# Sums of raw weights, attention's causal mask and half the rotations move from VectorE to GpSimd; inner operands are prepared in two pairs

## The chip, the cores and the metric

The kernel runs on one core of one Trainium2 chip. The metric is the device time of one execution in microseconds (us), the median of several. The engines are called as in the profile: PE (TensorE's matmuls) and PEld (its weight loads), DVE (VectorE), ACT (ScalarE), POOL (GpSimd), SP (SyncE, which issues the DMAs).

## What is computed

Two layers over 1024 tokens of width 1024 in float32. The first layer mixes by sliding-window attention with sinks, the second by a gated recurrence (HGRN2); each is followed by an MLP with a squared ReLU of inner width 4096. Cut to what matters here:

```python
# attention: blocks of 128 queries see their own block (causal) and the block before
q, k = apply_partial_rotary(q, cos, sin), apply_partial_rotary(k, cos, sin)   # 16 of 64 columns of a head
mask = (delta >= 0) & (delta < WINDOW) & (key_pos >= 0)
probs = softmax_with_sink(where(mask, q @ k.T * HEAD_DIM ** -0.5, NEG_INF), sink)
x = x + (probs @ v) @ w_o
...
# recurrence: q, f, i, g = split(h @ w_in, 4); chunks of 64 tokens with a carried state
...
# both layers
h = rmsnorm(x, mlp_norm[layer])
x = x + square(relu(h @ w_up[layer])) @ w_down[layer]
```

## The kernel before

Float32 accuracy is reached by three fast products: each operand is split into a high part (`wh` for weights, made by a cast on ACT or DVE) and a low part (`wl`, a subtraction on DVE), and `mm3` adds high x high, high x low and low x high. On top of that the large products are done by Strassen's scheme in Winograd's form: a 2 x 2 block product takes seven products instead of eight, and needs sums of blocks of the weights (s1 to s4) and of the activations.

`strassen_weights` loads four raw weight tiles of 128 x 512 (`wr`, by DMA), makes s1 = a10 + a11, s2 = s1 - a00, s3 = a00 - a10, s4 = a01 - s2 in tiles called `m`, and splits all of them into `wh` and `wl`. `pair` uses it for one pair of the up product's output tiles, 16 pairs in each layer; `two` uses it for the recurrence's projections, 12 times. From the fifth pair on, products 2 and 4 of a pair are not done directly: `inner` does them for two pairs at a time, ahead of use, by a second Strassen level on halves of 256 columns, with its own four half-width sums in each of 6 calls for each of the two products and each layer. `prepare` makes the activation sums that `inner` needs: it reads four kept tiles back by DMA, subtracts halves, splits three of the results and writes all of them to DRAM by DMA. `put_in` puts one more into place in pair 3 (pairs are counted from 0).

In attention, `attend_block` computes 4 heads x 128 queries x 256 keys, transposes the probabilities on PE, copies them to SBUF with ACT (`y`) and multiplies a copy by a 0/1 triangle `own_t` to keep keys up to the query (`own`); both feed the value products on PE. `rope` rotates a block's queries or keys by two products with the tables and a difference and a sum.

The order on each engine is not the written one. Every operation is recorded with the engines that may do it and a planned cost (`Schedule.add`); due times are worked back from PE's order, and a list scheduler (`Schedule.order`) then fills the engines by rank, with weight work given a lead. Where two engines may do an operation (casts to `wh`: ACT or DVE) it takes the one that looks better by the planned loads. Buffers come from small pools (`BUFS`): 6 `wr`, 5 `wh`, 5 `wl`, 7 `m`. On the chip each engine then runs its list in order. All instructions carry the line of the one call that issues them (L374), so they are told apart by tile names. PSUM banks are `p` and `q`, activation tiles `a` and `t`, DRAM tiles `d`, constants `c`.

Of the kernel before, what the change touches and what calls it, by code (L numbers as in the profile page):

```python
# [15 lines left out]
ALU = mybir.AluOpType  # L16
AX = mybir.AxisListType

P = 128
# [12 lines left out]
NG = 4  # L32
HD = 64
ROT = 16
# [9 lines left out]
LEVELS = 6  # L44
WARM = 10
INNER = (2, 4)
AT = 2
K_SPANS = ((-1, 3), (2, 6), (5, 8))

# [271 lines left out]
class Net:  # L321
# [88 lines left out]
        self.s.add({e: ways[e] for e in engines}, [out], [in_])  # L410

    def tt(self, e, out, x, y, alu, n=TH):
        cost = {"DVE": 70 + n * 1.04, "Pool": 147 + n * 2.105}
        engines = ("DVE",) if e == "any" else (e,)
        ways = {e: self.call(self.engine(e).tensor_tensor, out, x, y, alu) + (cost[e],) for e in engines}
        self.s.add(ways, [out], [x, y])
# [217 lines left out]
    def strassen_weights(self, first, second, done=()):  # L634

        self.s.lead = LEAD
        a = {(i, k): self.raw(src[:, k * TH : k * TH + TH]) for i, src in enumerate((first, second)) for k in range(2)}
        s1, s2, s3, s4 = (self.t(tag="m") for _ in range(4))
        self.tt("any", s1, a[1, 0], a[1, 1], ALU.add)
        self.tt("any", s2, s1, a[0, 0], ALU.subtract)  # L640
        self.tt("any", s3, a[0, 0], a[1, 0], ALU.subtract)
        self.tt("any", s4, a[0, 1], s2, ALU.subtract)
        order = ((1, a[0, 0]), (5, s1), (2, a[0, 1]), (6, s2), (3, s4), (7, s3), (4, a[1, 1]))
        w = {name: self.weight_split(z) for name, z in order if name not in done}
        self.s.lead = 0
        return w

    def prepare(self, name):

        near, far = slice(0, TH // 2), slice(TH // 2, TH)  # L650
        u = [self.t() for _ in range(HK)]
        for z, kept in zip(u, self.quarters[name]):
            self.dma(z, kept, 4 * P * TH)
        yield
        made = self.quarters[name] = {}

        def difference(out, x, y):
            for i in range(2):
                self.tt("any", out[:, i].only(i), x(i), y(i), ALU.subtract, TH // 2)

        def stored(k, t):
            made[k] = [self.keep(z.bitcast(F32)) for z in self.split(t.rearrange("p i c -> p (i c)"), self.t)]

        low, high = (lambda c: lambda i: u[i][:, c]), (lambda c: lambda i: u[2 + i][:, c])
        new = lambda: self.t(F32, (P, 2, TH // 2))
        part = lambda t: lambda i: t[:, i].only(i)
        t1 = new()
        difference(t1, low(far), low(near))
        made[5] = self.keep(t1.rearrange("p i c -> p (i c)"))
        yield  # L670
        t2 = new()
        difference(t2, high(far), part(t1))
        stored(6, t2)
        yield
        t3 = new()
        difference(t3, high(far), low(far))
        stored(7, t3)
        yield
        t4 = new()
        difference(t4, high(near), part(t2))  # L680
        stored(4, t4)
        yield
# [13 lines left out]
    def inner(self, name, m, x, y):  # L696
# [4 lines left out]
        a0, a1 = (self.raw(self.io["up"][self.layer, i + row * (MT // 2)][:, TH:]) for i in (m, m + 1))  # L701
        sa, sb = self.t(tag="m"), self.t(tag="m")
        s1, s2, s3, s4 = sa[:, near].only(0), sa[:, far].only(1), sb[:, near].only(0), sb[:, far].only(1)
        self.tt("any", s1, a1[:, near], a1[:, far], ALU.add, half)
        self.tt("any", s2, s1, a0[:, near], ALU.subtract, half)
        self.tt("any", s3, a0[:, near], a1[:, near], ALU.subtract, half)
        self.tt("any", s4, a0[:, far], s2, ALU.subtract, half)
        wide = []
        w = {1: (0, near), 2: (0, far), 5: (1, near), 6: (1, far), 7: (2, near), 3: (2, far), 4: (3, far)}
        self.s.lead = 0  # L710
        banks = [self.psum(), self.psum()]
        main, side, own = banks[0][:, near].only(0), banks[1][:, near].only(0), banks[1][:, far].only(1)

        def product(k, ps, start):
            more = {} if start else {"skip_group_check": True}
# [110 lines left out]
    def mlp(self, cut):  # L826

        x = self.mlp_second()
        made, n = {}, MT // 2
        for m in range(n):  # L830
            between, first = [], m - m % 2
            if m == AT:
                between += [self.prepare(name) for name in INNER]
            if m == AT + 1:
                between += [self.put_in(name, x[name]) for name in INNER]
            for name in INNER:
                c = first if name == 4 else first + 2
                if AT < c < n and m % 2 == (name == 2):
                    made[name, c] = []
                    between.append(self.inner(name, c, x, made[name, c]))  # L840
            done = {name: made[name, first][m % 2] if name == 2 else lambda: made[4, first][m % 2] for name in INNER if (name, first) in made}
            if m == n - 2:
                self.r = [self.a() for _ in range(NH)]
                for hf in range(NH):
                    self.copy(self.r[hf], self.spread(self.square[hf]))
            if m == 1 and self.layer == 0:
                self.hgrn_constants()
            self.pair(m, x, done, between)
        yield from self.down(cut)
# [175 lines left out]
        self.neg = self.const((P, 1))  # L1025
        self.memset(self.neg, NEG)

    def rope(self, x, heads, n):
        half = ROT // 2
        v = x.rearrange("p (h d) -> p h d", d=HD)[:, :, :ROT].rearrange("p h (a r) -> p h a r", a=2)  # L1030
        prod = []
        for tab in self.trig:
            y = self.t(F32, (P, 8, 2, half))[:, :heads]
            tb = tab[:, n].unsqueeze(1).unsqueeze(1).to_broadcast([P, heads, 2, half])
            self.tt("any", y, v, tb, ALU.mult, heads * ROT)
            prod.append(y)
        yc, ys = prod
        self.tt("any", v[:, :, 0], yc[:, :, 0], ys[:, :, 1], ALU.subtract, heads * half)
        self.tt("any", v[:, :, 1], yc[:, :, 1], ys[:, :, 0], ALU.add, heads * half)

    def k_tiles(self, i):
        if self.ks[i] is None:
# [34 lines left out]
    def projected(self, cg, n, ps, r):  # L1077
        if cg == 0:
            self.keys_values(n, ps, r)
        else:  # L1080
            q = self.a()
            self.stt(halves(q), straight(ps), r, halves(self.bias[cg]), ALU.mult, ALU.add)
            self.rope(q, 8, n)
            self.q[n][cg - 1] = q

    def keys_values(self, n, ps, r):
# [9 lines left out]
        if n:  # L1096
            before = self.v[(n - 1) // 2][:, (n - 1) % 2].only(n - 1)
            self.tt("any", self.dv[n // 2][:, n % 2].only(n), v, before, ALU.subtract, W)
        self.rope(k, NG, n)
        pk = self.psum("q")[:, : 2 * P].rearrange("p (g s) -> p g s", g=2)  # L1100
        for gp in range(2):
            self.transpose(pk[:, gp], k[:, gp * P : gp * P + P])
# [52 lines left out]
    def attend_block(self, g, n, stacks):  # L1155
# [30 lines left out]
        if n:  # L1186
            y = self.t(F32, (P, 4, P))
            self.copy(y, pt)
            self.tt("any", own, y, mask, ALU.mult)
            parts = [(y, self.v[(n - 1) // 2].only(n - 1)[:, (n - 1) % 2, g * HD : g * HD + HD]),  # L1190
                     (own, self.dv[n // 2].only(n)[:, n % 2, g * HD : g * HD + HD])]
        else:
            self.tt("DVE", own, pt, mask, ALU.mult)
            parts = [(own, v)]
# [536 lines left out]
```

## Time and profile before

| | |
|---|---|
| Time, median of 3 runs (lowest to highest) | 1993.26 us (1992.43 to 1994.49) |
| Profiled execution: time, span | 1992.46 us, 1990.6 us |
| Granted PE clock | 0.998 |
| DVE, ACT, POOL busy | 1763.1, 1108.4, 61.9 us |
| HBM traffic | 205 GB/s over the span |

An engine's busy time is set against the span. The profile has no stage names; by the tiles that are worked on, attention runs to about 330 us, the first up product to about 600, the first down product to about 1000, the recurrence to about 1350, with its output product and the second MLP behind it.

### The profile page before, as it was taken

To read this page: it belongs to the slowest core of one execution; us is meant where nothing else is said; L and a number is where in the kernel's file an instruction comes from. 1 tells how busy PE (TensorE), PEld (TensorE's weight loads), DVE (VectorE), ACT (ScalarE), POOL (GpSimd) and SP (SyncE) were. 2 spreads that over 40 slices of the span, in tenths; PEclk is the share of its full clock that TensorE was granted. 3 is DMA by queue.
4 is the path that set the end of the run, shared out by engine and by line. 5 is a ranking of instruction groups with operands and counts; after the bars stand their busy time and mean duration, and the time that the engine had idled before them with its cause. 6 is when DMAs were issued, how large, how long until landed. Compare 5 with 4: busy or idle time off the path is not lost.

```text
span 1990.6 us, 34667 instructions
## 1 busy us (share of the span) xinstructions
PE 1968.2 (99%) x11836; PEld 1723.3 (87%) x11836; DVE 1763.1 (89%) x3557; ACT 1108.4 (56%) x2280; POOL 61.9 (3%) x124
## 2 busy tenths in 40 slices
PE   9999999999999999999999999999999999999998
PEld 8877788899998888888888888888889998888887
DVE  8999899898889878899899999989989888987787
ACT  6567797666664423355455555554766666343352
POOL 4030000000000000000000000000000000000001
PEclk9999999999999999999999999999999999999999
DMA  6211464998889977755412212667599888986752
GB/s 224 90 54 59 127 217 162 308 304 290 285 264 319 330 244 244 242 167 179 140 59 81 75 60 86 206 203 253 185 313 305 285 278 280 317 315 211 239 173 85
DMA packets 232401, 411.04 MB, mean 206 GB/s; under 512 B 25504, under 2 KB 35744, under 8 KB 232224
## 3 DMA queue, kind: packets, MB, share of 16 engines
q1 hardware_dynamic: 231648, 408.30, 62.0%
q8 instruction: 93, 1.52, 0.3%
q14 instruction: 84, 0.69, 0.1%
q10 hardware_dynamic: 576, 0.52, 0.1%
HBM read 305.97 MB, written 102.76 MB: 205 GB/s over the span
## 4 chain that ended last, share of the span: by engine, by line
PE 89%; DVE 6%; issue 2%; ACT 2%; DMA 1%; POOL 0%; POOLq 0%; SPq 0%; DVEq 0%; ACTq 0%
PE q L374 51%; PE p L374 39%; DVE t L374 2%; DVE a L374 1%; DVE wl L374 1%; DVE m L374 1%; ACT t L374 1%; ACT a L374 1%; ACT wh L374 0%; ACT m L374 0%; DMA wr<-in_wo 0%; POOL a L374 0%; DMA wr<-in_up 0%; DMA a<-in_x 0%; DMA d<-t 0%
## 5 line engine op out<-in xcount | busy, mean ns | idle before, releaser
L374 PE MATMUL q<-a,wh 128*128 128x512 f32 x2368 | 708.4, 379 | 1.9 <-ACT t L374 1.6
L374 PE MATMUL p<-a,wh 128*128 128x512 f32 (+1 forms) x2304 | 657.7, 365 | 0.9 <-DVE wh L374 0.8
L374 PEld LDWEIGHTS q<-a,wh 128*128 128x128 f32 x2368 | 438.8, 189 | 59.2 <-ACT t L374 2.4
L374 PEld LDWEIGHTS p<-a,wh 128*128 128x128 f32 x2304 | 421.1, 189 | 55.4 <-issue 1.2
L374 PE MATMUL q<-a,wl 128*128 128x512 f32 x1184 | 448.1, 379 | 0.0
L374 PE MATMUL p<-a,wl 128*128 128x512 f32 (+1 forms) x1152 | 418.4, 364 | 0.0
L374 ACT CAST a<-t 128x512 fp32r<-128x512 f32 (+1 forms) x299 | 178.8, 613 | 216.8 <-PE q L374 126.6
L374 DVE TENSOR_TENSOR t<-t,t 128x512 f32<-128x512 f32 (+3 forms) x424 | 256.0, 628 | 11.6 <-ACT t L374 10.3
L374 PEld LDWEIGHTS q<-a,wl 128*128 128x128 f32 x1184 | 223.9, 189 | 30.3
L374 DVE TENSOR_TENSOR wl<-wr,wh 128x512 fp32r<-128x512 f32 (+1 forms) x352 | 233.8, 667 | 12.2 <-ACT wh L374 4.7
L374 PEld LDWEIGHTS p<-a,wl 128*128 128x128 f32 x1152 | 218.2, 190 | 25.1 <-issue 0.4
L374 DVE TENSOR_TENSOR a<-t,a 128x512 fp32r<-128x512 f32 (+2 forms) x334 | 218.4, 677 | 0.5 <-ACT a L374 0.2
L374 DVE TENSOR_TENSOR wl<-m,wh 128x512 fp32r<-128x512 f32 x296 | 201.6, 684 | 7.6 <-ACT wh L374 4.0
L374 ACT CAST wh<-wr 128x512 fp32r<-128x512 f32 x221 | 131.7, 598 | 136.1 <-PE p L374 46.2
L374 ACT ACTIVATE t<-t 128x512 f32<-128x512 f32 x296 | 183.7, 630 | 35.7 <-DVE t L374 23.5
L374 ACT CAST wh<-m 128x512 fp32r<-128x512 f32 x239 | 147.0, 618 | 89.5 <-PE p L374 38.8
L374 ACT COPY t<-q 128x512 f32<-128x512 f32 (+3 forms) x190 | 105.2, 557 | 63.8 <-PE q L374 59.3
L374 DVE CAST wh<-wr 128x512 fp32r<-128x512 f32 (+1 forms) x131 | 55.0, 419 | 89.2 <-PE q L374 67.2
L374 ACT COPY t<-p 128x256 f32<-128x256 f32 (+1 forms) x157 | 70.5, 452 | 95.4 <-PE p L374 78.0
L374 DVE TENSOR_TENSOR m<-wr,wr 128x512 f32<-128x512 f32 x184 | 118.8, 649 | 3.8 <-DMA wr<-in_down 3.5
L374 PE MATMUL p<-wh,a 128*128 128x512 f32 x352 | 110.9, 385 | 0.0
L374 PEld LDWEIGHTS q<-t,t 128*64 128x64 f32 (+1 forms) x2160 | 95.5, 144 | 14.0 <-issue 6.3
(138 smaller groups left out, 2330.4 us busy)
## 6 DMA issues: line engine op xcount, KB each, us to landing
t<-d SPq DMA_DIRECT2D x428, 256.0 KB, 4.4
d<-t SPq DMA_DIRECT2D x312, 256.0 KB, 4.1
wr<-in_down SPq DMA_DIRECT2D x256, 256.0 KB, 4.2
wr<-in_up SPq DMA_DIRECT2D x176, 256.0 KB, 4.4
a<-d SPq DMA_DIRECT2D x60, 256.0 KB, 4.9
wr<-in_wqkv SPq DMA_DIRECT2D x48, 256.0 KB, 2.9
d<-a SPq DMA_DIRECT2D x48, 256.0 KB, 3.3
wr<-in_win SPq DMA_DIRECT2D x48, 256.0 KB, 2.9
```

The source lines that it names most:

```text
L374: fn(*[place(a) for a in args], **{k: place(v) for k, v in kw.items()})
```

## The change

Five edits. The four sums of `strassen_weights` and of `inner` are given to POOL instead of DVE. POOL's planned cost of such an operation goes from 147 + 2.105 n to 212 + 3.0 n ns for n columns. `prepare` runs in pair 1 for product 2 and in pair 2 for product 4, where both ran in pair 2 (with it, the record of what was made is set up before the first step). The rotation of the queries of the second half's blocks goes to POOL; keys and the first half stay on DVE. The own-block mask becomes an index selection on POOL (keep where query index minus key index is not negative) in every block but the first. The banks of `inner` are tracked whole instead of by halves.

```diff
 INNER = (2, 4)
+PREPARED = {2: 1, 4: 2}
...
     def tt(self, e, out, x, y, alu, n=TH):
-        cost = {"DVE": 70 + n * 1.04, "Pool": 147 + n * 2.105}
+        cost = {"DVE": 70 + n * 1.04, "Pool": 212 + n * 3.0}
...
     def strassen_weights(self, first, second, done=()):
-        self.tt("any", s1, a[1, 0], a[1, 1], ALU.add)
-        self.tt("any", s2, s1, a[0, 0], ALU.subtract)
-        self.tt("any", s3, a[0, 0], a[1, 0], ALU.subtract)
-        self.tt("any", s4, a[0, 1], s2, ALU.subtract)
+        self.tt("Pool", s1, a[1, 0], a[1, 1], ALU.add)
+        self.tt("Pool", s2, s1, a[0, 0], ALU.subtract)
+        self.tt("Pool", s3, a[0, 0], a[1, 0], ALU.subtract)
+        self.tt("Pool", s4, a[0, 1], s2, ALU.subtract)
...
     def inner(self, name, m, x, y):
-        self.tt("any", s1, a1[:, near], a1[:, far], ALU.add, half)
+        self.tt("Pool", s1, a1[:, near], a1[:, far], ALU.add, half)
...
-        main, side, own = banks[0][:, near].only(0), banks[1][:, near].only(0), banks[1][:, far].only(1)
+        main, side, own = banks[0][:, near], banks[1][:, near], banks[1][:, far]
...
-            if m == AT:
-                between += [self.prepare(name) for name in INNER]
+            between += [self.prepare(name) for name, at in PREPARED.items() if m == at]
...
     def projected(self, cg, n, ps, r):
-            self.rope(q, 8, n)
+            self.rope(q, 8, n, "DVE" if n < BPH else "Pool")
...
     def attend_block(self, g, n, stacks):
-            self.tt("any", own, y, mask, ALU.mult)
+            self.op("Pool", self.nc.gpsimd.affine_select, [own], [y], 750, own, y, [[0, 4], [1, P]], ALU.is_ge, 0.0,
+                    base=0, channel_multiplier=-1)
```

Three places in the built order. First, DVE before at the start of the first up product; the weight sums (`m`) stand between the splits (`wl`) and the activations' sums (`t`).

```order
L374 TENSOR_TENSOR wl_3909<-wr_3772,wh_3896 128x512
L374 TENSOR_TENSOR m_3916<-wr_3824,wr_3855 128x512
L374 TENSOR_TENSOR t_3763<-t_3763,t_3699 128x512
L374 TENSOR_TENSOR a_3931<-p_3862,t_3663 128x512
L374 TENSOR_TENSOR wl_3936<-wr_3795,wh_3922 128x512
L374 TENSOR_TENSOR m_3945<-m_3916,wr_3795 128x512
L374 TENSOR_TENSOR t_3708<-t_3941,t_3708 128x512
L374 TENSOR_TENSOR t_3884<-t_3884,t_3948 128x512
L374 TENSOR_TENSOR m_3969<-wr_3806,m_3945 128x512
L374 TENSOR_TENSOR wl_3976<-m_3916,wh_3961 128x512
```

The same pair's place on DVE now, where a cast to `wh` stands that ACT did before:

```order
L375 TENSOR_TENSOR wl_3955<-wr_3789,wh_3941 128x512
L375 TENSOR_TENSOR t_3889<-t_3889,t_3947 128x512
L375 CAST wh_3972<-m_3907 128x512
L375 TENSOR_TENSOR t_3889<-t_3889,t_3953 128x512
L375 TENSOR_TENSOR wl_3983<-m_3907,wh_3972 128x512
L375 TENSOR_TENSOR t_3889<-t_3889,t_3961 128x512
```

And on POOL now, two pairs' sums in one row, s3, s1, s2, s4 of each:

```order
L375 TENSOR_TENSOR m_3877<-wr_3789,wr_3839 128x512
L375 TENSOR_TENSOR m_3907<-wr_3839,wr_3863 128x512
L375 TENSOR_TENSOR m_3930<-m_3907,wr_3789 128x512
L375 TENSOR_TENSOR m_3958<-wr_3813,m_3930 128x512
L375 TENSOR_TENSOR m_3980<-wr_3893,wr_3924 128x512
L375 TENSOR_TENSOR m_4009<-wr_3924,wr_3966 128x512
```

The sums have left DVE's row; over the whole program 181 casts (156 of 512 columns, 25 of 256) have come to it from ACT.

Second, DVE before in the pair where both preparations ran: the halves' differences (128x256) of both products, mixed with weight sums and splits.

```order
L374 TENSOR_TENSOR m_4599<-wr_4520,wr_4531 128x512
L374 TENSOR_TENSOR t_4536<-t_4492 128x256
L374 TENSOR_TENSOR t_4612<-t_4484 128x256
L374 TENSOR_TENSOR wl_4618<-wr_4307,wh_4602 128x512
L374 TENSOR_TENSOR t_4612<-t_4504 128x256
L374 TENSOR_TENSOR t_4627<-t_4468,t_4536 128x256
L374 TENSOR_TENSOR t_4627<-t_4543,t_4536 128x256
L374 TENSOR_TENSOR m_4635<-m_4599,wr_4307 128x512
L374 TENSOR_TENSOR m_4644<-wr_4307,wr_4520 128x512
```

DVE now, in the pair before that one, with the differences of one product alone:

```order
L375 TENSOR_TENSOR t_4447<-t_4322 128x256
L375 TENSOR_TENSOR t_4447<-t_4302 128x256
L375 CAST wh_4461<-m_4237 128x512
L375 TENSOR_TENSOR wl_4468<-m_4237,wh_4461 128x512
L375 TENSOR_TENSOR t_4474<-t_4408,t_4447 128x256
L375 TENSOR_TENSOR t_4478<-t_4408,t_4322 128x256
L375 TENSOR_TENSOR t_4474<-t_4424,t_4447 128x256
```

The eight differences of one product have moved a pair ahead; those of the other follow 20 rows later on the same engine.

Third, attention, while the second half's queries are projected. DVE before: rotations (products with the tables `c_430` and `c_453`) and the mask (product with `c_103`) among the softmax's steps.

```order
L374 TENSOR_TENSOR t_1982<-a_1869,c_430 128x128
L374 TENSOR_TENSOR t_1985<-t_1971,c_103 128x512
L374 COPY_PREDICATED m_1422<-c_98,q_1966 128x2x128
L374 TENSOR_TENSOR t_1999<-a_1869,c_453 128x128
L374 TENSOR_TENSOR t_2003<-a_1891,c_430 128x128
L374 TENSOR_TENSOR a_1869<-t_1982,t_1999 128x8x8
```

POOL now, at the same place:

```order
L375 TENSOR_TENSOR t_1949<-a_1926,c_430 128x128
L375 TENSOR_TENSOR t_1961<-a_1926,c_453 128x128
L375 TENSOR_TENSOR a_1912<-t_1929,t_1936 128x8x8
L375 AFFINE_SELECT t_1975<-t_1958 128x512
L375 TENSOR_TENSOR a_1912<-t_1929,t_1936 128x8x8
L375 TENSOR_TENSOR t_1997<-a_1956,c_430 128x128
```

The selection of one block stands between the steps of a rotation in POOL's row, so it starts only when those ahead of it have run.

More of the change, by code (lines that the diff above doesn't have):

```diff
@@ L653, in prepare @@
             self.dma(z, kept, 4 * P * TH)
+        made = self.quarters[name] = {}
         yield
-        made = self.quarters[name] = {}
         def difference(out, x, y):
@@ L703, in inner @@
         s1, s2, s3, s4 = sa[:, near].only(0), sa[:, far].only(1), sb[:, near].only(0), sb[:, far].only(1)
-        self.tt("any", s1, a1[:, near], a1[:, far], ALU.add, half)
-        self.tt("any", s2, s1, a0[:, near], ALU.subtract, half)
-        self.tt("any", s3, a0[:, near], a1[:, near], ALU.subtract, half)
-        self.tt("any", s4, a0[:, far], s2, ALU.subtract, half)
+        self.tt("Pool", s1, a1[:, near], a1[:, far], ALU.add, half)
+        self.tt("Pool", s2, s1, a0[:, near], ALU.subtract, half)
+        self.tt("Pool", s3, a0[:, near], a1[:, near], ALU.subtract, half)
+        self.tt("Pool", s4, a0[:, far], s2, ALU.subtract, half)
         wide = []
@@ L1026, in attention_constants, with rope @@
         self.memset(self.neg, NEG)
-    def rope(self, x, heads, n):
+    def rope(self, x, heads, n, e):
         half = ROT // 2
@@ L1034, in rope @@
             tb = tab[:, n].unsqueeze(1).unsqueeze(1).to_broadcast([P, heads, 2, half])
-            self.tt("any", y, v, tb, ALU.mult, heads * ROT)
+            self.tt(e, y, v, tb, ALU.mult, heads * ROT)
             prod.append(y)
         yc, ys = prod
-        self.tt("any", v[:, :, 0], yc[:, :, 0], ys[:, :, 1], ALU.subtract, heads * half)
-        self.tt("any", v[:, :, 1], yc[:, :, 1], ys[:, :, 0], ALU.add, heads * half)
+        self.tt(e, v[:, :, 0], yc[:, :, 0], ys[:, :, 1], ALU.subtract, heads * half)
+        self.tt(e, v[:, :, 1], yc[:, :, 1], ys[:, :, 0], ALU.add, heads * half)
     def k_tiles(self, i):
@@ L1098, in keys_values @@
             self.tt("any", self.dv[n // 2][:, n % 2].only(n), v, before, ALU.subtract, W)
-        self.rope(k, NG, n)
+        self.rope(k, NG, n, "DVE")
         pk = self.psum("q")[:, : 2 * P].rearrange("p (g s) -> p g s", g=2)
```

## The prediction

> **What bounds the kernel now.** I read the page's busy times first, then stretches by stage, then waits, then the groups that the change touches.
>
> ```profile
> PE 1968.2 (99%) x11836; PEld 1723.3 (87%) x11836; DVE 1763.1 (89%) x3557; ACT 1108.4 (56%) x2280; POOL 61.9 (3%) x124
> ```
>
> TensorE (PE) is idle for 1990.6 - 1968.2 = 22.4 us in all, and the change adds or removes no matmul. So the most it can win is a part of these 22.4 us; what it can lose has no such limit. The stretches show where they lie (columns after the length: busy us and count of PE, PEld, DVE, ACT, POOL, then clock, DMA share, GB/s):
>
> ```profile
> 50.00:150.00 100.00, 96.02 (x535) 78.42 (x535) 92.48 (x221) 61.45 (x182) 18.17 (x33) 1.00 0.23 71
> 150.00:250.00 100.00, 98.59 (x617) 79.02 (x616) 88.86 (x197) 72.22 (x240) 5.75 (x16) 1.00 0.30 93
> 250.00:350.00 100.00, 99.79 (x517) 85.11 (x516) 98.52 (x215) 79.17 (x178) 0.36 (x2) 1.00 0.58 194
> 350.00:390.00 40.00, 38.24 (x193) 33.25 (x192) 35.76 (x73) 25.33 (x47) 0.00 (x0) 1.00 0.93 314
> 390.00:600.00 210.00, 210.00 (x1207) 190.21 (x1206) 181.98 (x346) 139.32 (x271) 0.00 (x0) 1.00 0.87 285
> ...
> 1000.00:1350.00 350.00, 346.65 (x3391) 303.83 (x3391) 319.47 (x733) 199.06 (x392) 8.27 (x18) 1.00 0.36 115
> ...
> 1450.00:1490.00 40.00, 39.07 (x211) 34.33 (x210) 34.31 (x67) 28.08 (x54) 0.00 (x0) 1.00 0.92 313
> ...
> 1960.00:1990.60 30.60, 21.27 (x181) 20.73 (x179) 17.70 (x50) 5.28 (x14) 5.26 (x6) 0.88 0.39 137
> ```
>
> Idle PE: attention (50 to 350) 3.98 + 1.41 + 0.21 = 5.6 us; early in the first up product (350 to 390) 1.76 and in the second (1450 to 1490) 0.93; the recurrence's stage (1000 to 1350) 3.35; the tail 9.3, which the change hardly enters. So about 11.6 us are within its reach. Two more things stand here: 250 to 350 has the Vector engine (DVE) at 98.5% and PE still at 99.8%, so a nearly full DVE is not yet a late PE; and in the recurrence DVE has 30 us left of 350.
>
> The waits of PE in 50 to 350 name DVE for 5.1 of the 5.6 us:
>
> ```profile
> PE q L374 <- DVE a L374: 2.5, 6, 0.7
> PE q L374 <- DVE m L374: 2.4, 4, 1.3
> PE q L374 <- DVE t L374: 0.2, 1, 0.2
> ```
>
> The timeline of the first up product shows its two large waits, at the place where the inner products begin, just after both preparations stood in one pair:
>
> ```profile
> 376.27 0.71 PE L374 MATMUL p<-a,wh 128*128 128x256 f32 x4 [0.75 <-DVE wh L374]
> 377.69 0.70 PE L374 MATMUL q<-a,wh 128*128 128x512 f32 x2 [0.70 <-ACT t L374]
> ```
>
> **The change, part by part.** The prices of what leaves DVE, and of the casts that come to it:
>
> ```profile
> L374 DVE TENSOR_TENSOR m<-wr,wr 128x512 f32<-128x512 f32 x160 | 108.7, 684 | 3.8 <-DMA wr<-in_down 3.5
> L374 DVE TENSOR_TENSOR m<-wr,wr 128x256 f32<-128x256 f32 x24 | 10.0, 417 | 0.0
> L374 DVE TENSOR_TENSOR t<-t,c 128x512 f32<-128x512 f32 x28 | 19.2, 686 | 0.5 <-ACT t L374 0.4
> L374 DVE TENSOR_TENSOR t<-a,c 128x128 f32<-128x128 f32 x32 | 8.3, 283 | 0.0
> L374 DVE TENSOR_TENSOR a<-t,t 128x64 f32<-128x64 f32 x32 | 6.7, 216 | 0.2
> L374 DVE CAST wh<-m 128x512 fp32r<-128x512 f32 x57 | 24.2, 425 | 20.5 <-PE q L374 16.0 <-PE p L374 3.9
> ```
>
> By the two built orders, 176 sums of 512 columns go to GpSimd (POOL): 32 pairs and 12 projections by 4, 176 x 0.684 = 120 us; 96 of 256 columns, 40 us; 28 masks, 19 us; half the rotations, 16 x 0.283 + 16 x 0.216 = 8 us. The planner, seeing DVE free, gives it 156 casts of 512 and 25 of 256 columns that ScalarE (ACT) had: 66 and about 7 us. So DVE's own work goes from 1763 to about 1649 us. ACT gets shorter, which is worth nothing at 56%.
>
> What comes to POOL is bounded by the nearest rows:
>
> ```profile
> L374 POOL TENSOR_TENSOR a<-a,t 128x512 f32<-128x512 f32 x2 | 2.5, 1286 | 657.8 <-ACT t L374 657.8
> L374 POOL TENSOR_TENSOR a<-a,t 128x256 f32<-128x256 f32 x4 | 2.8, 730 | 21.4 <-ACT t L374 21.4
> L374 POOL TENSOR_SCALAR_AFFINE_SELECT c<-t 128x128 f32<-128x128 f32 x1 | 0.3, 292 | 0.1
> ```
>
> These ran beside DVE work on PSUM, so they are the undisturbed price: 1.29 and 0.73 us. The select of 512 columns lies between 0.29 (the row itself) and four times it, 1.17; I take 0.8, since a fixed start is in the row. Rotations by the slope of the two sums, 2.2 ns a column: 0.45 and 0.31 us, 1.5 us for one rotation against 1.0 on DVE; their queries are wanted only by the second half's attention, so that costs nothing, as long as the masks behind them in POOL's queue are not late.
>
> The open price is what the two engines do to each other. The trace has it in small:
>
> ```profile
> 32.75 0.89 POOL L374 TENSOR_SCALAR a<-a 64x128 fp32r<-64x128 f32 x1 [10.05 <-ACT a L374]
> 32.43 0.18 DVE L374 TENSOR_TENSOR t<-t,t 128x32 f32<-128x32 f32 x1
> 32.53 0.68 DVE L374 TENSOR_TENSOR wl<-wr,wh 128x512 fp32r<-128x512 f32 x1
> 33.13 0.31 DVE L374 TENSOR_TENSOR t<-t,t 128x32 f32<-128x32 f32 x1
> 33.37 0.41 DVE L374 TENSOR_TENSOR a<-a 128x256 f32<-128x256 f32 x1
> ...
> 113.38 0.51 DVE L374 TENSOR_TENSOR a<-a 128x256 f32<-128x256 f32 x1
> ...
> 208.93 0.77 POOL L374 TENSOR_SCALAR m<-c 128x4 f32<-128x4 f32 x1 [5.50 <-DVE sm L374]
> 208.93 0.69 DVE L374 TENSOR_TENSOR m<-m,sm 128x512 f32<-128x512 f32 x1
> ...
> 1039.16 1.56 POOL L374 TENSOR_SCALAR a<-t 128x512 f32<-128x512 f32 x1 [25.21 <-ACT t L374]
> 1040.17 0.68 DVE L374 TENSOR_TENSOR wl<-wr,wh 128x512 fp32r<-128x512 f32 x1
> ```
>
> POOL waits: an operation on four columns took 0.77 us, as long as the DVE sum beside it; the one at 32.75 ended 0.43 us after the DVE sum at 32.53 did. DVE then pays a little: the sum of 128x32 took 0.31 instead of 0.18 behind it, and the one at 113.38 took 0.51 instead of 0.41 for the same shape, so 0.10 to 0.13 us for a read of 128 columns. But the DVE sum at 1040.17 took its 0.68 with a 512-column POOL operation under way until 1040.72. So a POOL sum of 2 x 512 columns costs DVE between 0 (that row) and 8 x 0.13 = 1.0 us (every column read at that toll). I take 0.4, nearer the low end: the toll shows only where a POOL read starts behind a DVE operation, and in 1.3 to 2 us two to four of DVE's operations end. That is 176 x 0.4 + 96 x 0.2 = 90 us, with 6 for the selects, and DVE ends near 1745 us: hardly lighter than before. POOL gets 176 x (1.3 to 2.0) + 96 x (0.7 to 1.1) + about 40, so 330 to 500 us more.
>
> An up product alone (350 to 600, 250 us): DVE 35.8 + 182.0 = 218 us; 64 x 0.684 + 48 x 0.417 = 64 leave, about 70 casts of 512 and 13 of 256 come (34): 188, and with the tolls 188 + 64 x 0.4 + 48 x 0.2 = 223, or 89% against 87%. I cost it at nothing there. What covers it is that the engines that split weights wait for PE to hand weight buffers back, in this stage:
>
> ```profile
> DVE wh L374 <- PE q L374: 25.8, 14, 2.4
> ACT wh L374 <- PE q L374: 18.3, 28, 1.6
> ```
>
> The weights are ready ahead, by 1.8 us at a mean DVE wait. The chain s1, s2, s4 takes 3 x 1.3 to 2.0 us in place of 3 x 0.68, 2 to 4 us later, and raw buffers are held as much longer; the planner has put the splits behind it. If that cover were gone, the excess of about 1 us would fall on each of 32 pairs, 32 us. At the head of the up products one preparation moves a pair earlier: same instructions, DMAs included, spread over two pairs. The idle 1.76 + 0.93 = 2.7 us stands there; I take 2.0, since a part (a wait for a DMA'd operand) may stay. The coarser bookkeeping of the two inner banks only adds a PE wait for a DVE read that lies a whole product back: nothing.
>
> In attention DVE loses 27 us, gains 10 casts (4 us) and tolls (28 x 0.2 and a little for the rotations, 8 us): 15 us net of 280. The mask itself comes later, by 0.1 us and what POOL waits, 0 to 0.7; it is behind a copy and ahead of a value product for which other matmuls stand ready. I take half of the 5.1 us of PE's waits for DVE: 2.5. In the recurrence 48 x 0.684 = 33 us leave, 20 casts (8.5) and tolls of 48 x 0.4 = 19 come: a quarter of 3.35, 0.8.
>
> Sum: 2.0 + 2.5 + 0.8 = 5.3 us off the span of 1990.6. The profiled execution took 1992.46, 0.8 under the median of 1993.26, and 1.9 of it lies around the span. Against the median: 1988.0.
>
> **Rivals.** *DVE fills up.* At the high end, 1.0 us a sum wherever DVE reads two SBUF operands, and DVE's PSUM sums and casts are about a fifth of its time here: 188 + 64 x 0.8 + 48 x 0.4 = 258 us in 250, so each up product gets some 8 to 10 us longer and the kernel 1988 + 20 = 2008. It decides from a toll of about 0.87 us a sum, where 188 + (64 + 24) x 0.81 x 0.87 reaches 250. For it: POOL and DVE do wait for each other above. Against it: the row at 1040.17. If a POOL sum shut DVE out for its whole 1.29 us, 188 + 64 x 1.04 + 48 x 0.59 = 283, which is +33 us for each up product and 2059 in all. [...]
>
> *Nothing to measure.* PE is full, the removed waits come back one product later or as a mask that is late in POOL's queue behind a rotation: 1993. For it: only 11.6 us are in reach at all, and DVE's load barely falls.
>
> *The sums are late.* The 32 us above: 2020. Against it stand 25.8 us of waiting for buffers.
>
> **Chances.** Forecast (1983 to 1989, centre 1988) 0.46; nothing, 0.28; DVE fills up 0.16, the full block 0.04; late sums 0.06. Under 0.2% (4 us) this kernel's measurement can't tell from no change. Faster 0.46, same 0.28, slower 0.26. Low end: 11 us of the 11.6 in reach, 1982; high end: the filled DVE at 2008.
>
> **What would show it.** Right: PE's waits at the first inner products gone; POOL sums of 512 columns at 1.5 to 2.0 us, DVE sums at 0.70 to 0.80 in the up products with DVE at 88 to 93% and PE at 100%. Wrong: DVE sums of 0.9 us or more and PE waiting for DVE wl or ACT wh in 390 to 600; or PE waits in attention on a POOL tile.

## The result, and the profile after

The changed kernel takes 2171.76 us (median of 4 runs, 2167.77 to 2173.2) against 1992.85 us for the kernel before on the same chip: a ratio of 1.0893, 95% interval 1.0874 to 1.0912. That is 179 us slower and far outside the predicted range of 1982 to 2008. The profiled execution took 2172.28 us, with a span of 2170.3 us at a granted clock of 0.97.

The page of the changed kernel begins with the busy times (share of the span, instructions); its clock row has one digit for each fortieth of the span:

```profile
PE 2031.2 (94%) x11836; PEld 1760.7 (81%) x11836; DVE 1845.1 (85%) x3406; ACT 1019.9 (47%) x2099; POOL 441.9 (20%) x456
...
PEclk9999999998999999999999999999999989999999
```

PE does the same 11836 matmuls. Its idle time went from 22.4 to 2170.3 - 2031.2 = 139.1 us, and its busy time grew by 63.0 us, which a number of matmuls that stays the same can only do by running slower. The two make up the 179.7 us of the spans. No engine is full: DVE has a lower share than before, 85% against 89%.

The stretches say where (columns as in the prediction: length, then busy us and count of PE, PEld, DVE, ACT, POOL, then clock, DMA share, GB/s):

```profile
50.00:150.00 100.00, 95.23 (x534) 77.78 (x533) 88.83 (x215) 60.22 (x180) 23.86 (x46) 1.00 0.22 69
150.00:250.00 100.00, 98.96 (x626) 79.97 (x626) 84.54 (x165) 70.54 (x243) 28.09 (x59) 1.00 0.31 96
250.00:350.00 100.00, 89.69 (x440) 74.45 (x439) 91.95 (x154) 60.41 (x136) 32.43 (x19) 0.93 0.49 163
350.00:390.00 40.00, 34.47 (x151) 28.45 (x151) 38.06 (x92) 20.96 (x39) 8.70 (x9) 0.98 0.74 259
390.00:600.00 210.00, 179.97 (x931) 157.67 (x930) 162.93 (x246) 83.23 (x158) 80.44 (x72) 0.92 0.70 223
700.00:750.00 50.00, 50.00 (x233) 43.80 (x232) 47.62 (x84) 20.31 (x33) 0.00 (x0) 1.00 0.93 321
```

In 390 to 600, all of it the first up product, PE idles 30 of 210 us where it idled none, the clock is 0.92, and DVE's busy time falls to 78% of the stretch. In the down product (700 to 750) POOL has nothing to do and PE is full at clock 1.00.

Set matmul against matmul (the k-th of before against the k-th of after, by their start times), the delay grows like this:

| Matmul that started in before at | later by |
|---|---|
| 250 us (attention) | -0.6 us |
| 318 us (attention ends, first splits) | +15.6 |
| 600 us (end of the first up product) | +84.9 |
| 1000 us (end of the down product) | +85.7 |
| 1350 us (recurrence) | +100.1 |
| 1450 us (its output product) | +117.4 |
| 1680 us (end of the second up product) | +180.1 |
| the end of the span | +179.7 |

The time goes in the stages in which POOL makes sums; the down product, which has none, loses nothing. The largest waits (total us, times, longest), by what PE waited for, and who kept ACT and DVE waiting:

```profile
PE p L375 <- ACT wh L375: 68.6, 18, 3.8
PE q L375 <- DVE t L375: 21.3, 10, 5.9
...
ACT t L375 <- DVE t L375: 271.1, 146, 6.0
...
DVE wh L375 <- PE q L375: 144.6, 136, 3.3
```

In the kernel before, ACT's waits for `t` were less than a third of that:

```profile
ACT t L374 <- DVE t L374: 83.2, 83, 3.1
```

PE waits most for ACT's casts, ACT waits for DVE's sums `t`, and DVE, later in the pair, waits for PE. That loop is why all three show idle time. One pair of the first up product shows a full turn. This is the timeline (start, length, then engine and work; "x2" two instructions together; in brackets the idle time ahead and its releaser); rows of the same engines in between that are not needed are left out:

```profile
507.86 2.98 POOL L375 TENSOR_TENSOR m<-wr,wr 128x512 f32<-128x512 f32 x2 [6.00 <-DVE wl L375]
...
508.03 1.65 DVE L375 TENSOR_TENSOR t<-t,t 128x512 f32<-128x512 f32 x1
...
509.60 0.41 DVE L375 TENSOR_TENSOR t<-p,t 128x256 f32<-128x256 f32 x1
...
509.94 1.45 DVE L375 TENSOR_TENSOR wl<-m,wh 128x512 fp32r<-128x512 f32 x1
...
510.91 1.61 POOL L375 TENSOR_TENSOR m<-m,wr 128x512 f32<-128x512 f32 x1
...
511.31 1.49 DVE L375 CAST wh<-m 128x512 fp32r<-128x512 f32 x1
...
512.60 1.35 POOL L375 TENSOR_TENSOR m<-wr,m 128x512 f32<-128x512 f32 x1
512.72 1.78 DVE L375 TENSOR_TENSOR t<-t,t 128x512 f32<-128x512 f32 x1
...
514.53 1.29 ACT L375 ACTIVATE t<-t 128x512 f32<-128x512 f32 x2 [3.39 <-DVE t L375]
...
515.73 0.60 ACT L375 CAST wh<-wr 128x512 fp32r<-128x512 f32 x1
...
516.39 0.49 PE L375 MATMUL p<-a,wh 128*128 128x256 f32 x2 [3.83 <-ACT wh L375]
```

POOL runs a pair's four sums in one burst of 6.1 us. In it DVE gets five instructions through. Four of them have operands in SBUF alone and take 1.65, 1.45, 1.49 and 1.78 us, against 0.68, 0.69, 0.43 and 0.68 undisturbed: 3.9 us more, about 1.0 for each sum. The fifth, with an operand in PSUM (`p`), keeps its 0.41. The sum `t` that ends at 514.50 is what ACT's activation waits for; the cast of the next weight tile stands behind two activations in ACT's list, and PE waits 3.83 us for that cast. The same wait comes back in ten pairs of the first up product, 3.80 us on average, and 15 waits of over 0.3 us there take 46.1 us (before: 3 and 1.8).

The groups of the changed kernel (busy us, mean ns of one | idle us ahead of the group):

```profile
L375 DVE TENSOR_TENSOR t<-t,t 128x512 f32<-128x512 f32 x311 | 262.0, 862 | 6.4 <-ACT t L375 5.3 <-issue 0.3
...
L375 DVE CAST wh<-m 128x512 fp32r<-128x512 f32 x173 | 103.3, 597 | 60.0 <-PE q L375 41.0 <-PE p L375 15.4 <-POOL m L375 2.7
...
L375 DVE TENSOR_TENSOR t<-q,t 128x512 f32<-128x512 f32 x60 | 40.7, 680 | 0.0
...
L375 POOL TENSOR_TENSOR m<-wr,wr 128x512 f32<-128x512 f32 x88 | 138.5, 1587 | 845.3 <-DVE a L375 386.3 <-DMA wr<-in_up 164.3 <-DVE wl L375 133.1
```

The first of these groups before:

```profile
L374 DVE TENSOR_TENSOR t<-t,t 128x512 f32<-128x512 f32 x311 | 206.4, 683 | 8.7 <-ACT t L374 7.9
```

These means hide two kinds. Every DVE instruction of the trace, sorted by whether a POOL sum of 256 columns or more ran beside it for over 0.1 us:

| DVE instruction | alone, us (count) | beside a POOL sum, us (count) |
|---|---|---|
| two operands in SBUF, 512 columns | 0.687 (1505) | 1.287 (144), a tenth over 1.77 |
| cast, 512 columns | 0.434 | 1.239 (46), half over 1.49 |
| two operands in SBUF, 256 columns | 0.439 | 0.872 |
| one operand in PSUM, 512 columns | 0.683 | 0.678 |

All of it together is 141 us over 272 sums, 0.52 us a sum.

What the busy PE lost stands behind the waits. After that of 3.83 us:

```profile
516.71 0.60 PE L375 MATMUL q<-a,wh 128*128 128x512 f32 x2
...
518.42 0.42 PE L375 MATMUL p<-a,wl 128*128 128x256 f32 x1
...
520.34 1.03 PE L375 MATMUL q<-a,wh 128*128 128x512 f32 x2
521.20 0.39 PE L375 MATMUL q<-a,wl 128*128 128x512 f32 x1
521.42 0.59 PE L375 MATMUL q<-a,wh 128*128 128x512 f32 x2
```

From 517.8 to 521.2 a matmul of 256 columns comes every 213 ns instead of 111, and one of 512 every 427 instead of 216: half rate. By the clock that the trace grants, PE is busy at half rate for 40.8 us of the first up product, which costs half of that, 20.4 us, and for 37.8 us of the second, which costs 18.9; in the kernel before neither has any.

### The profile page after: what moved, and what is told of

Same layout as the page of the kernel before. It is cut to its first block, busy times and chain, and to the rows that moved or that the text cites. A ratio compares the mean times of both kernels' runs of the same rounds, so it can differ in the third digit from the quotient of the medians.

```text
span 2170.3 us, 34964 instructions
## 1 busy us (share of the span) xinstructions
PE 2031.2 (94%) x11836; PEld 1760.7 (81%) x11836; DVE 1845.1 (85%) x3406; ACT 1019.9 (47%) x2099; POOL 441.9 (20%) x456
## 5 line engine op out<-in xcount | busy, mean ns | idle before, releaser
L375 PE MATMUL p<-a,wh 128*128 128x512 f32 (+1 forms) x2304 | 677.2, 376 | 78.6 <-ACT wh L375 68.6
L375 PE MATMUL q<-a,wh 128*128 128x512 f32 x2368 | 724.7, 388 | 10.2 <-ACT t L375 9.9
L375 POOL TENSOR_TENSOR m<-wr,wr 128x512 f32<-128x512 f32 (+1 forms) x112 | 158.4, 1424 | 845.3 <-DVE a L375 386.3
L375 DVE TENSOR_TENSOR t<-t,t 128x512 f32<-128x512 f32 (+3 forms) x424 | 318.5, 777 | 9.8 <-ACT t L375 7.7
L375 ACT CAST a<-t 128x512 fp32r<-128x512 f32 x291 | 175.6, 617 | 225.7 <-PE q L375 121.7
L375 DVE TENSOR_TENSOR wl<-m,wh 128x512 fp32r<-128x512 f32 x296 | 226.5, 766 | 22.1 <-PE q L375 12.6
L375 DVE CAST wh<-wr 128x512 fp32r<-128x512 f32 (+1 forms) x178 | 84.9, 477 | 117.5 <-PE q L375 89.9
L375 ACT CAST wh<-wr 128x512 fp32r<-128x512 f32 x174 | 106.7, 616 | 118.1 <-PE p L375 48.9
L375 DVE CAST wh<-m 128x512 fp32r<-128x512 f32 x173 | 103.3, 597 | 60.0 <-PE q L375 41.0
L375 PE MATMUL q<-t,t 128*64 128x32 f32 (+2 forms) x2160 | 105.7, 230 | 8.7 <-ACT t L375 4.5
```

Source lines behind the costliest of these rows:

```text
L375: fn(*[place(a) for a in args], **{k: place(v) for k, v in kw.items()})
```

## The experiments

| Kernel | Median us | Ratio to before, 95% interval |
|---|---|---|
| after | 2171.76 | 1.0893 [1.0874, 1.0912] |
| e1_sums_dve: after, sums back on DVE | 1993.77 | 1.0001 [0.9992, 1.0011] |
| e2_only_sums: before, only the sums on POOL | 2163.94 | 1.0852 [1.0830, 1.0873] |
| e3_fill: after, POOL writes in place of summing | 2013.38 | 1.0097 [1.0082, 1.0112] |
| e4_dead_reads: e1, with idle sums on POOL | 2176.69 | 1.0915 [1.0894, 1.0937] |
| e5_prepared: before, preparation in two pairs | 1993.28 | 1.0003 [0.9994, 1.0012] |
| e6_attention: before, mask and rotations on POOL | 1996.71 | 1.0018 [1.0009, 1.0027] |
| e7_pieces: after, sums in 128-column pieces | 2092.59 | 1.0501 [1.0481, 1.0521] |
| e8_one_sum: after, one sum of four on POOL | 2020.13 | 1.0137 [1.0118, 1.0156] |
| e9_prep_consts: e5, constants later | 1988.63 | 0.9976 [0.9967, 0.9985] |
| e10_told: after, the planner knows the toll | 2052.95 | 1.0297 [1.0278, 1.0316] |
| e11_half_fill: e3 with half the writing | 2007.32 | 1.0072 [1.0057, 1.0088] |
| e12_consts_only: before, constants later | 1991.68 | 0.9994 [0.9985, 1.0003] |

### Which part of the change: e1_sums_dve and e2_only_sums

```diff
# e1_sums_dve, from the kernel after (strassen_weights and inner)
-        self.tt("Pool", s1, ...)      # and s2, s3, s4
+        self.tt("any", s1, ...)
# e2_only_sums, from the kernel before: the same lines the other way,
# and POOL's planned cost as in the kernel after
```

> The changed kernel with all sums of raw weights back on DVE; the preparation in two pairs, attention's mask and rotations on POOL stay. Exclusion (a POOL operation that reads two SBUF operands shuts DVE's two-operand work out for its whole length, four in a row make DVE some 4 us late in each pair, ACT's queue stands behind DVE and PE behind ACT): the whole loss goes, 1985 to 1995 us, and the 4 us waits of PE before the first inner product of every pair are gone. Other parts of the change as the cause (earlier preparation, mask, banks tracked whole): a good part of the 179 us stays, over 2030 us.

> The kernel before with only the sums of raw weights on POOL at the new planned cost. Exclusion: nearly the whole loss, 2140 to 2180 us, with DVE sums of 1.4 to 1.8 us wherever they run beside a POOL sum. Other parts as the cause: under 2060 us.

The sums alone bring the loss, and without them it is gone: 2163.94 and 1993.77 us. e1 also shows the rest of the change by stage; its stretches:

```profile
250.00:350.00 100.00, 96.87 (x487) 82.08 (x486) 94.55 (x205) 67.74 (x151) 9.16 (x7) 0.98 0.57 188
```

In 350 to 390 and 1450 to 1490 its PE is busy 40.00 and 39.63 us (38.24 and 39.07 before), but in 250 to 350 it has lost 2.9 of the 99.79 us. The rest of the change wins and loses about the same.

### What it is about the sums: e3_fill and e4_dead_reads

The first theory: a POOL instruction that reads SBUF shuts DVE out, one instruction at a time. Its rivals: the sums are late, since each takes twice as long and starts a chain; or DVE's new list, with 181 more casts, is simply a worse order. e3 keeps every list and every dependence and takes away POOL's reading. e4 has DVE make the sums as before, and POOL read the same tiles for nobody.

```diff
# e3_fill, from the kernel after: what each of the four sums issues on POOL
-            tensor_tensor(out, x, y, alu)
+            tensor_tensor(out[:, :4], x[:, :4], y[:, :4], alu)
+            memset(out[:, 4:], 0.01)      # twice
# e4_dead_reads, from e1_sums_dve (strassen_weights; one buffer of a fewer for the dead tile)
+        for x, y in ((a[1, 0], a[1, 1]), (a[0, 0], a[1, 0]), (a[0, 0], a[0, 1]), (a[0, 1], a[1, 1])):
+            self.tt("Pool", self.dead, x, y, ALU.add)
```

> The changed kernel in which each POOL sum reads only its first four columns and then fills the rest of its tile twice with a constant (the weight sums are left out, so the output is not the reference's): nearly as long on POOL (about 1.2 us for 512 columns against 1.27 undisturbed), same waits, and the same order on every other engine. Exclusion by reads: DVE's two-operand sums return to 0.69 us beside them, PE's waits go, under 2020 us. Late sums (the chain on POOL as such delays the splits) or the new order (181 casts that came from ACT): all of it stays, 2150 us or more. If DVE's casts are held by writes too, a part stays, 2030 to 2080 us.

> The weight sums of the pairs and projections on DVE, and beside them four POOL sums for each pair that read the same raw tiles into a tile nobody reads (one activation buffer fewer makes room for it; sums of half width stay on DVE alone). Exclusion: the loss comes back though nobody waits for a POOL result but the raw buffers, 2100 us or more, DVE sums of 1.4 to 1.8 us in the bursts. Late sums: nothing to be late for, 1990 to 2010 us.

e3_fill, with the same order on PE, DVE, ACT and SP and POOL as busy (439.0 us), loses 20 us instead of 179. Its groups on DVE, and its stretch of the first up product:

```profile
L375 DVE TENSOR_TENSOR t<-t,t 128x512 f32<-128x512 f32 x311 | 205.6, 681 | 7.3 <-ACT t L375 6.2 <-issue 0.2
...
L375 DVE CAST wh<-m 128x512 fp32r<-128x512 f32 x173 | 90.7, 524 | 40.9 <-PE q L375 25.1 <-PE p L375 11.3 <-POOL m L424 3.9
```

```profile
390.00:600.00 210.00, 206.34 (x1172) 181.54 (x1172) 164.00 (x307) 103.04 (x198) 96.85 (x264) 1.00 0.84 270
```

DVE's sums are back at 681 ns, and PE's 18 waits for ACT's `wh`, 68.6 us in the kernel after, have shrunk to 6.5. So neither the order nor the lateness of the sums costs much by itself: the two up products lose 8.4 and 8.5 us with both, and with POOL's writes. A part stays: casts beside the writing take 0.683 us instead of 0.434, so casts, unlike sums, are held by POOL's writes too.

e4_dead_reads takes 2176.69 us, the whole loss, though no instruction waits for what POOL makes and DVE's `wh<-m` casts are only 54. Its groups:

```profile
L376 DVE TENSOR_TENSOR t<-t,t 128x512 f32<-128x512 f32 x311 | 251.5, 827 | 6.7 <-ACT t L376 6.0 <-issue 0.5
...
L376 POOL TENSOR_TENSOR c<-wr,wr 128x512 f32<-128x512 f32 x176 | 280.8, 1595 | 1090.8 <-DMA wr<-in_up 549.6 <-DMA wr<-in_win 513.2 <-DMA t<-d 9.6
```

Lateness and casts are out as the cause: POOL reading SBUF beside DVE is enough. The dead reads also keep raw buffers for longer, but the other engines wait no more than 2.3 us for the up products' raw weights in this run. (In e4 DVE has the sums as well, so the equal total is no measure of size.)

e11_half_fill writes once instead of twice.

> The run with fills again, with one fill instead of two (the weight sums are left out here too; same order on all other engines). If its 20 us over the kernel before come half from writes that hold DVE's casts: 2000 to 2007 us, with casts beside a fill at 0.6 to 0.7 us. If they come from the new order and attention alone: 2013.

It took 2007.32 us, 0.3 above what was expected, 6 us under e3, and casts beside a fill took 0.73 us on average, also above what was expected. So a part of e3's 20 us grows with the time POOL writes; whether through the casts that it holds or through tiles that are ready later, this run does not part. With attention's 4 us (e6, below) some 10 us are left for the shorter writing, the order and the waits for POOL; they were not split further.

### How it reaches PE: e7_pieces, e8_one_sum, e10_told

```diff
# e7_pieces, from the kernel after
-            tensor_tensor(out, x, y, alu)
+            for c in range(0, n, 128):
+                tensor_tensor(out[:, c : c + 128], x[:, c : c + 128], y[:, c : c + 128], alu)
# e8_one_sum, from the kernel after: s1, s2, s4 and inner's sums back to "any"
         self.tt("Pool", s3, a[0, 0], a[1, 0], ALU.subtract)
# e10_told, from the kernel after (Schedule.order, with form="sum" on these operations)
             free_at[e] = t + cost
+            if e == "Pool" and op.form == "sum":
+                free_at["DVE"] = max(free_at.get("DVE", 0.0), t) + 0.6 * cost
```

> The changed kernel with each POOL sum issued in pieces of 128 columns (same planned cost and order). Exclusion held for one instruction at a time: no DVE sum of 512 columns takes 1.4 us or more on account of one piece, they take 0.68 plus one piece of 0.45, 1.0 to 1.2 us, but over a stretch three to four times as long; the pieces keep DVE out for 16 x 4 x 4 x 0.45 us in each up product alone, and the time is as bad or worse, 2150 to 2250 us. Sharing by bandwidth instead of by instruction: same DVE times as with whole sums, and 2150 to 2180.

e7_pieces was expected to be as bad or worse, since the same columns are read with four times the starts. It took 2092.59 us: a miss, and a telling one. Its groups:

```profile
L375 DVE TENSOR_TENSOR wl<-m,wh 128x512 fp32r<-128x512 f32 x296 | 216.8, 733 | 12.0 <-ACT wh L375 1.3 <-DVE wh L375 0.5 <-PE q L375 0.4
...
L420 POOL TENSOR_TENSOR m<-wr,wr 128x128 f32<-128x128 f32 x400 | 281.0, 733 | 693.5 <-DVE a L375 373.0 <-DMA wr<-in_up 137.0 <-DVE m L375 93.6
```

Now the pieces wait for DVE (0.73 us each instead of 0.45), and DVE's sums of 512 columns take 0.85 us on average beside a piece (some 440 of them, 0.69 alone), with a tenth over 0.946; none takes 1.4 or more, and none the 1.0 to 1.2 that was expected. So an instruction waits for the other engine's instruction under way, and a short one is a short wait: DVE is held for 0.3 us at most beside a piece, which takes 0.45 us undisturbed, and for 1.1 us beside a whole sum, which takes 1.27. PE's largest wait for `wl` is 2.4 us, and the first up product has 8.3 us of busy PE at half rate instead of 40.8. About 100 us remain. DVE's instructions still lose some 110 us in all beside the pieces (141 beside whole sums), and POOL is busy for longer (705.5 us); how the 100 us divide was not tested.

> The changed kernel with one sum of four on POOL (s3 of each pair and projection, 44 instructions), the others and inner's on DVE. The loss comes from bursts that outrun the weight buffers' lead of 1.8 us: one sum makes DVE about 1 us late and is covered, 1992 to 2005 us. The loss goes by the number of sums: a quarter of the 160 us of the 176, 2030 us or more.

e8_one_sum also missed, between its two theories: 2020.13 us. Set matmul against matmul with e1_sums_dve, which has the rest of the change too, sixteen single sums cost the two up products 8.1 and 7.8 us, 0.5 us a sum; all of them, in the kernel after, cost 71 and 64 us in a stage of 64 sums and 48 half sums, 0.73 to 0.81 for 512 columns. A single sum holds DVE for 0.56 us on average in this run, so little of that is covered, and four in a row cost about one and a half times as much each. The lists differ as well (DVE has 289 casts here, 420 in the kernel after), so this run does not part the burst from the order.

> The changed kernel with a planner that keeps DVE busy for 0.6 of a POOL sum's planned cost (1.05 us for 512 columns) from the start of each sum, so that the order knows of the exclusion; the built order gives DVE 246 casts instead of 420. If the loss is that the order gives DVE work that it then hasn't time for: most of it goes, 2010 to 2080 us. If the DVE time that the sums take is missing whatever the order: 2120 us or more.

e10_told changes no work: the planner alone is told that DVE stands still for 0.6 of a sum's planned cost. 2052.95 us, within what was expected, and 119 of the 179 us are back. It gives DVE 246 casts instead of 420. The first up product in its stretches:

```profile
390.00:600.00 210.00, 200.18 (x1128) 176.13 (x1128) 168.10 (x232) 128.00 (x252) 107.34 (x88) 1.00 0.80 266
```

PE is busy 200 of 210 us instead of 180, ACT has 128 us of work instead of 83, and POOL even more than in the kernel after. The sums hold DVE nearly as much as there, 0.47 us a sum against 0.52, yet PE waits far less. So two thirds of the loss was a list made for a DVE that has more time than it has. What remains, 60 us, this plan did not find cover for.

### The smaller parts: e6_attention, e5_prepared, e9_prep_consts, e12_consts_only

```diff
# e6_attention: the kernel before with rope and attend_block of the kernel after
# e5_prepared, from the kernel before
-            if m == AT:
-                between += [self.prepare(name) for name in INNER]
+            between += [self.prepare(name) for name, at in PREPARED.items() if m == at]
# e9_prep_consts: e5_prepared and this; e12_consts_only: the kernel before and this
-            if m == 1 and self.layer == 0:
+            if m == 6 and self.layer == 0:
                 self.hgrn_constants()
```

> The kernel before with only attention's part of the change: the mask by index selection and half the rotations on POOL. The prediction's term: 2.5 us faster, 1990.7. What the run with the sums on DVE shows: 4 to 5 us slower, 1997 to 1999, with one selection that stands some 5 us on POOL while DVE runs two-operand work without a gap, and PE waits of DVE t near it.

e6_attention: 1996.71 us, 4 us slower than before. By matmuls it is ahead by 1.2 us at 250 us and behind by 6.0 at 318. Of these 7 us, 4.8 come between 266 and 270 us, where PE has its two largest waits, for steps of the softmax on DVE:

```profile
PE q L374 <- DVE t L374: 1.6, 1, 1.6
PE q L374 <- DVE m L374: 1.4, 1, 1.4
```

They end at 267.28 and 269.58 us. PE's new list has no other matmul between these steps, and from 269.9 us the clock is at half for 6.83 us. Why the lists of PE and DVE meet like this was not looked for. The long select that was expected to cost the time begins only at 269.08 us, when these waits are nearly over. The timeline of the kernel after has the same place:

```profile
269.69 6.18 POOL L375 TENSOR_SCALAR_AFFINE_SELECT t<-t 128x512 f32<-128x512 f32 x2 [4.75 <-ACT t L375]
...
270.91 3.69 DVE L375 TENSOR_TENSOR a<-a,a 128x512 fp32r<-128x512 f32 x6
...
275.15 0.97 PEld L375 LDWEIGHTS q<-t,a 128*64 128x64 f32 x10 [0.61 <-POOL t L375]
```

Undisturbed, most selects take 0.63 us. Here two take 6.18, the first of them until DVE's row of six sums without a gap is over, and a weight load waits 0.61 us for the result. The hold goes both ways: beside these gapless DVE instructions POOL does not get in. Beside another such row, at 338.99, a POOL sum took 6.24 us.

> The kernel before with only the preparation spread over pairs 1 and 2. The prediction's term: the waits at the first inner products go, 2.0 to 2.7 us of 1993, so 1990 to 1991. Rival: the waits come back elsewhere, 1993.

e5_prepared changed nothing that can be measured. The two waits at 376 to 378 us are gone, and two others have come in pair 1:

```profile
358.17 0.70 PE L375 MATMUL q<-a,wh 128*128 128x512 f32 x2 [0.68 <-DVE wh L375]
...
359.90 0.99 PE L375 MATMUL q<-a,wh 128*128 128x512 f32 x2 [1.03 <-ACT t L375]
...
361.11 1.06 PE L375 MATMUL q<-a,wh 128*128 128x512 f32 x2
```

They are followed by half rate until 363 us (two matmuls in 1.06 instead of 0.59), and the kernel is 3.3 us behind at the matmul of 390 us. In pair 1 of the first layer `hgrn_constants` runs too. So the next two kernels move it to pair 6. (The crowded pair alone does not decide it: e1_sums_dve has preparation and constants in pair 1 as well, and its PE is busy for all of 350 to 390.)

> The kernel with only the preparation spread over pairs 1 and 2, and the recurrence's constants (some 40 small DVE operations, first layer only) made in pair 6 instead of pair 1. If the new waits of 2 us and the half-rate stretch behind them at 357 to 363 us come from preparation and constants in one pair, they go: 1989 to 1991 us. If they come from the preparation in pair 1 as such, they stay: 1993.

> The kernel before, with nothing but the preparation of the recurrence's constants (hgrn_constants, first layer) moved from pair 1 to pair 6; prepare stays in pair 2 for both products. It splits the 4.5 us that e9_prep_consts gained. If the gain is the preparation's, which the constants only hid in e5_prepared, this kernel keeps the waits of 0.75 + 0.70 us at 376 to 378 us and those at 1450 to 1490, and takes 1992 to 1994 us. If the constants in pair 1 were by themselves what cost time before, it takes 1988 to 1990 us with PE at 40.0 of 40 us in 350 to 390. In between (1990 to 1992) each has a share, the second up product's 0.9 us staying with the preparation in any case.

e9_prep_consts takes 1988.63 us, 4.5 us under before and faster than both kernels. e12 splits that gain. By matmuls, the constants' move alone wins 2.2 us at 390 us (e9: 2.6), so the waits there were those of a crowded DVE, and one piece of work less in the pair was enough. At the head of the second up product, where no constants stand, e12 wins nothing and keeps its 39.07 of 40 us, while e9 has:

```profile
1450.00:1490.00 40.00, 39.89 (x222) 35.87 (x221) 35.92 (x72) 26.85 (x52) 0.00 (x0) 1.00 0.93 317
```

There e5 and e9 both win 1.3 us, the preparation's own. In the trace of e12, 1.9 of its 2.2 us are lost again in the recurrence (1050 to 1350), for a reason not looked for, and its median cannot be told from before. The trace of e9 loses 1.8 us at the same place and ends 2.3 us ahead of before; that execution was 1.3 us above e9's median, so the 4.5 us are not accounted for in full.

## Why the prediction was wrong

The step that failed is "I cost it at nothing there", for the up products. By matmuls they lost 69 and 63 us. It went wrong in three places.

**The toll as a mean.** Taken: 0.4 us a sum, DVE at 89% of an up product's time, so no loss. The mean over the kernel is not far off, 0.52 us. But a sum does not slow DVE by a share: it stops one instruction for about 1.0 us, and sums come four in a row. What PE saw was 3.8 us at once, pair after pair, and a stage average of 89% says nothing of that. My high end also took DVE's casts as free of the toll, like its sums on PSUM; 46 of them took 1.24 us instead of 0.43. The same holds for the two rivals that I worked out from loads: "DVE fills up" (10 us an up product) and the full block (33 us) are sums of busy time too, and the stage lost 69 us without DVE being full.

**The row at 1040.17.** I let one row, a DVE sum at 0.68 beside a POOL operation, outweigh the rows where each waits for the other, and gave the full block a chance of 0.04. It was the mechanism: beside a POOL sum DVE's two-operand instructions of 512 columns took up to 1.80 us instead of 0.687. (Its price, 2059, was set on the 1993 of before, that of the filled DVE, 2008, on the forecast's 1988.) The DVE sum of that row starts 1.01 us into POOL's operation. The kernel after has the same operation with two DVE instructions beside it, the first from 0.08 us into it, the second from 1.08:

```profile
1131.82 1.50 POOL L375 TENSOR_SCALAR a<-t 128x512 f32<-128x512 f32 x1 [0.31 <-ACT t L375]
...
1131.90 1.07 DVE L375 TENSOR_TENSOR wl<-wr,wh 128x512 fp32r<-128x512 f32 x1
...
1132.90 0.68 DVE L375 TENSOR_TENSOR t<-t,t 128x512 fp32r<-128x512 f32 x1
```

The first is held by 0.39 us, the second is not. So an operation with one operand holds DVE as well (beside the selects, two-operand instructions took up to 1.12 us), but in these rows only early in its time (from 0.08 us into it, not from 1.01 or 1.08), and the row at 1040.17 showed the part behind that. Measured in these runs, for 512 columns: a DVE instruction with two inputs in SBUF took 0.687 us alone and up to 1.80 beside a POOL sum, and POOL's sum 1.27 alone and up to 6.24; a DVE instruction with an input in PSUM took 0.683 alone and 0.678 beside a sum; and with POOL's writes in place of its sums (e3_fill) DVE's sums took 0.681.

**The cover.** Taken: engines that split weights wait for PE, 1.8 us at a mean wait, so the weights are ready ahead. That time is real but is not behind the burst: ACT's list has the next weight cast behind an activation that waits for DVE, so a late DVE `t` makes a late `wh`, and a 3.9 us hold is longer than 1.8 us in any case. e8_one_sum shows that even a single sum's hold is hardly covered. The rival "the sums are late" had 1 us a pair; e3_fill shows lateness to be a small part.

To this the half-rate stretches came, some 39 us in the two up products, which no step had.

The other terms:
- Attention, -2.5 us: the sign was wrong, +4 us (e6_attention). The step failed at "for which other matmuls stand ready": at 266 to 270 us none stood ready, PE waited 1.4 and 1.6 us for DVE, and half rate followed. "0 to 0.7" for what POOL waits was wrong too: it waited up to 5 us behind DVE's gapless rows, though PE saw only 0.6 of that. The price of the select, 0.8 us, was good (0.63 undisturbed, 0.88 on average).
- Preparation, -2.0 us: half right. The removed waits are gone as I said, 1.3 us of it at the second up product in e5 and e9. At the first one the step left out the cost of a pair that is crowded already, and the edit alone gains nothing (e5_prepared); what e9 wins there, the constants' move wins nearly alone (2.2 of 2.6 us), and most of that is lost again in the recurrence.
- Recurrence, -0.8 us: +14 us in the kernel after, and nothing lost there in e1_sums_dve, so the sums cost it; its waits were not followed one by one.
- DVE at 1745 us: 1845. The toll accounts for half of the difference (141 us instead of 90, by the table above); the rest I did not trace to a group.
- POOL's sums at 1.3 to 2.0 us: 1.37 to 1.59 on average, as taken.
- What was to show the prediction wrong did: "DVE sums of 0.9 us or more and PE waiting for DVE wl or ACT wh in 390 to 600".

## What to carry to other kernels

In this kernel GpSimd's sums read SBUF, and in a burst each stopped one VectorE instruction with its operands there for about 1.0 us; those with an operand in PSUM were not stopped (0.683 us alone, 0.678 beside a sum). So before work goes from VectorE to GpSimd, look at where the operands lie, and count the price per burst at the place where it falls, against the lead there, not as a share of a stage's load. Shorter instructions and a planner that knows the stop took a part of it back (79 and 119 of 179 us), not all. When work is moved to another place in the order, ask first what that place has too much of already.

## What the hardware showed that was not expected

- A cast on DVE is held by POOL's reads and by its writes: 0.434 us alone, 1.239 beside sums, 0.683 beside fills; a two-operand sum only by the reads: 0.687 alone, 1.287 beside sums, 0.681 in e3_fill.
- In the bursts, with work queued on both, they take turns, one instruction each (four sums and four DVE instructions on SBUF alone from 507.86 to 514.50 us in the kernel after); beside some DVE rows without gaps POOL gets no turn (a select of 5.41 us, a sum of 6.24). What decides between the two no run here shows.
- PE fell to half rate after waits that I had not thought to matter. Of the 23 waits of 2.4 us or more in the kernel after, all but two are met or followed by half rate. In that trace the clock falls to half only at points of a grid of 3.413 us, and stays there for one to three such intervals (the stretch that ends with the span apart). In its up products it fell after every interval at full rate in which PE had idled for 57.7% or more (1.97 us), and after none with 57.0% or less. So it matters where a wait falls: the two that no half rate followed lay across two intervals, at 55 and 57% of each. Shorter waits can add up: in e5_prepared 0.68 and 1.03 us in the 3.4 us ahead of it, half of that time, were followed by half rate (357 to 360 us). Among the smaller matmuls of the recurrence it fell after an interval with 37% (1190 us in the kernel after). What sets the limit no run here shows.
